# Sample attention in groups of four sequences, and later emission of norm multiplies, convolution steps and masked products, in a hybrid attention and state-space step

## The chip, the cores and the metric

The kernel runs on one core of one Trainium2 chip. The metric is the device time of one execution in microseconds; the median of runs counts.

## The reference

One layer of a decoder trunk with two groups of heads, on 512 prompt tokens and on 64 sample tokens (8 sequences of 8). Everything is fp32.

```python
h = rmsnorm(x, norm_pre)
q, k, v, g_a, z, xbc, dt = split(h @ w_in)
# group A: sliding-window attention (128), 32 query heads on 4 kv heads, a learned sink per head
o_a = attend(q, k, v, mask, sink)        # prompt: blocks of 128; sample: 128 cached keys + 8 new
attn_out = rmsnorm(o_a * silu(g_a), attn_norm)
# group B: Mamba-2 SSD
xbc = silu(causal_conv(xbc, conv_w, conv_b))         # width 4, depthwise
y, h_new = ssd(xs, dt, A, B, C, h0)                  # chunks of 128 with masked decay products
ssm_out = rmsnorm((y + d_skip * xs) * silu(z), ssm_norm)   # in 4 groups
out = concat(attn_out, ssm_out) @ w_out
return x + rmsnorm(out, norm_post), new caches and states
```

For the sample part, `swa_step` puts the 8 new keys behind the 128 cached ones; with T=8, W=128 query t sees key s where 0 <= t + 128 - s < 128. So of the cached keys it sees those with index above t, and of the new keys those with index up to t: always 128 keys.

## The kernel before

Tokens stand in columns: 512 prompt and 64 sample, 576 in two halves of 288; features stand in the 128 partitions. Every weight block (128 rows by 512 columns, a "unit") is loaded to one of 9 `raw` buffers, split into a high part (ACT cast, line 329) and a low part (DVE subtraction, line 332) in one of 4 `w` buffers, and used by `mm3` (lines 348 to 350): three fp32r matmuls, high by high, high by low, low by high. Where two column tiles are projected together (`pair`), seven products take the place of eight, with sums of weights made on POOL (line 269) and sums of results on DVE (lines 414 to 420).

The order is: x is normed while the first tiles are projected; the xBC tiles of four SSM groups and the z tiles; then for each of two rounds (pr = 0, 1; two kv heads each) k, v and eight pairs of q and gate tiles; then two output passes over w_out, the SSM half first, the attention half second. The projections are the dense work of TensorE. All else is side work.

The order of all instructions is made in advance. `Schedule` holds tasks written as generators; each `mm3` is a tick, and `yield n` means "go on n ticks later". A task emits its instructions at its tick into the in-order queues of the engines, and one DMA queue on SP takes all transfers. So a `yield` between a producer and its consumer sets how much other work stands ahead of the consumer on its engine; it is no wait in itself. If a task or a projection can get no buffer, it spends ticks until there is one. Buffers of 576 columns come from one pool (`slots`, with `smalls` a view on it), PSUM has 8 `banks`.

What the diff touches:

- `qb_task` (prompt attention, one call per head pair and half): scores, row maximum, exp, scaling, transposes, then ACT copies the transposed weights out of PSUM (line 1010) and DVE multiplies the same bank by a triangle mask (lines 1012 and 1014, the masked products), then the value matmuls (line 1024).
- `smp_task` (sample attention, one per round): loads of cached keys and values into four buffers; then `one(b)` for each of 8 sequences, at most three in flight. The kv heads stand in partition halves, so scores are 64-row matmuls for each half (lines 1067, 1068), two masked maxima with an additive mask tile (1074, 1075), exp (1081), scaling (1086), two transposes (1090, 1091), two copies (1094, 1095) and the value matmuls for each half, cached keys and new keys (1101, 1102) into one PSUM bank `osb` for all 8. At the end one multiplication by the gate for all (1115), stores to `m_d` and square sums.
- `renorm` (line 1129; called four times for the SSM groups and once for the 16 blocks of attention): `factors` loads the reciprocal norms (written to `r_d` by `Sums.finish`, 8 ticks before); then per block a load from `m_d` (1135), 8 ticks later the multiply on DVE (1137), one tick later the store (1139). The output passes read `m_d` (line 1544) once a block is ready.
- `conv_task` (line 1157, 24 calls): ACT makes the first tap (1163), three DVE steps add the others (1166), ACT tanh (1168), DVE finishes.
- `seq` inside `sample` (line 1374 on): the SSM state of a sequence is updated by DVE (1385) two ticks behind its matmul (1382).

Of the kernel before, what the change touches and what calls it, by code (L numbers as in the profile page):

```python
# [16 lines left out]
P = 128  # L17
# [161 lines left out]
def kern(ctx: ExitStack, tc: tile.TileContext, a: dict, o: dict):  # L179
# [15 lines left out]
    def const(name, shape):  # L195
        t = sb("c_" + name, shape)
        dma(t, a[name])
        return t
# [476 lines left out]
    masks = const("masks", [P, 640])  # L675
# [261 lines left out]
    def qb_task(st, jj, m, u):  # L937
# [72 lines left out]
        S.copy(pT[1][:, :512], pt)  # L1010
        if f:
# [5 lines left out]
        yield 9  # L1017
# [28 lines left out]
    def smp_task(st):  # L1046

        pr = st.pr
        own, ck, cv = [], [], []
        for h in range(2):  # L1050
            for src, dst in (("ckT", ck), ("cv", cv)):
                t = yield from smalls.get()
                own.append(t)
                dst.append(t[:, :512].rearrange("p (b k) -> p b k", b=4))
                dma(dst[h], a[src][pr, :, 4 * h:4 * h + 4])
        yield from wait(lambda: len(st.q) == 8 and st.kready and st.vready)
        if pr:
            yield 75
        osb = yield from banks.get()
        done = []  # L1060

        def one(b):
            sc = yield from banks.get()
            for hf in range(2):
                r0 = slice(64 * hf, 64 * hf + 64)
                lq = st.qs[r0, 64 * b:64 * b + 64]
                PE.matmul(sc[r0, 0:128], lq, ck[b // 4][r0, b % 4], start=True, stop=True)
                PE.matmul(sc[r0, 128:192], lq, st.kn[r0, TP:T], start=True, stop=True)
            yield 1
            pslot = yield from smalls.get()  # L1070
            p_ = pslot[:, :192]
            tn = yield from tiny.get()
            m0, mx, nm, den, es = (tn[:, k:k + 1] for k in range(5))
            V.tensor_tensor_reduce(p_[:, :128], sc[:, :128], masks[:, :128], 1.0, -3e38, ALU.add, ALU.max, m0)
            V.tensor_tensor_reduce(p_[:, 128:], sc[:, 128:192], masks[:, 128 + 64 * b:192 + 64 * b], 1.0, m0,
                                   ALU.add, ALU.max, mx)
            banks.put(sc)
            V.scalar_tensor_tensor(nm, mx, -0.125, nsinks[:, pr:pr + 1], op0=ALU.mult, op1=ALU.min)
            V.tensor_tensor(es, nm, sinks[:, pr:pr + 1], ALU.add)
            yield 3  # L1080
            S.activation(p_, p_, AF.Exp, bias=nm, scale=0.125, accum_out=den)
            S.activation(es, es, AF.Exp)
            yield 3
            V.tensor_tensor(den, den, es, ALU.add)
            V.reciprocal(den, den)
            V.tensor_scalar(p_, p_, den, None, op0=ALU.mult)
            tiny.put(tn)
# [721 lines left out]
```

## Time and profile before

| | us |
|---|---|
| median of 3 runs | 1655.22 (1653.7 to 1661.37) |
| profiled execution | 1653.8 |
| its span | 1652.0 |
| PE busy in it | 1598.8 (97%) |
| DVE busy | 1095.8 (66%) |
| ACT busy | 771.1 (47%) |
| POOL busy | 389.4 (24%) |

A matmul's time runs from its start to its modelled end and overlaps the next one's, so times of single matmuls do not add up; the step from start to start does. PEclk is the granted TensorE clock as a share of 2.4 GHz; it is either 1 or one half at any moment, and a figure between is a mean over the stretch. A wait is put down to the last releaser.

### The profile page before, as it was taken

The page shows a single profiled execution, that of the slowest core. Times are in us where ns is not written, and L with a number is a line of the kernel's source. Part 1 is how long each engine was busy: PE and PEld are TensorE (multiplying, and loading weights), DVE is VectorE, ACT ScalarE, POOL GpSimd, SP SyncE. Part 2 cuts the span into 40 slices and gives each one's busy share as a digit, 9 for nine tenths or more (in the row PEclk, how much of TensorE's full clock was granted, in tenths as well). Part 3 has the DMA queues.
Part 4 walks back from the last instruction along what each step waited for, and adds up shares of the span by engine and source line. Part 5 has one row for each costly group of instructions (what it writes and reads, how often), then busy time and mean ns, then how long its engine had stood idle before and what let it go on. Part 6 is the DMA issues. An engine that isn't in the chain of part 4 may idle for free.

```text
span 1652.0 us, 31869 instructions
## 1 busy us (share of the span) xinstructions
PE 1598.8 (97%) x12158; PEld 1542.6 (93%) x12158; DVE 1095.8 (66%) x2185; ACT 771.1 (47%) x1849; POOL 389.4 (24%) x420
## 2 busy tenths in 40 slices
PE   8999999999999999999999999999999999999995
PEld 8899999999989998998999999999899999999995
DVE  7656755775667567476778868777686455655556
ACT  6433433444434445364655636656573322544440
POOL 3201222221312220342223213222111211023323
PEclk9999999999999999999999999999999999999997
DMA  6324356546565648446314322323461356723235
GB/s 238 89 74 110 90 180 187 146 163 188 142 154 160 186 131 279 132 134 135 103 58 126 87 75 75 97 71 109 132 201 46 96 153 216 271 86 103 91 100 186
DMA packets 157977, 222.98 MB, mean 135 GB/s; under 512 B 32160, under 2 KB 66080, under 8 KB 157792
## 3 DMA queue, kind: packets, MB, share of 16 engines
q1 hardware_dynamic: 157824, 220.95, 44.5%
q8 instruction: 95, 1.56, 0.4%
q14 instruction: 58, 0.48, 0.1%
HBM read 182.26 MB, written 40.60 MB: 135 GB/s over the span
## 4 chain that ended last, share of the span: by engine, by line
PE 80%; DVE 8%; DMA 6%; ACT 2%; issue 2%; SPq 1%; POOL 0%; DVEq 0%; ACTq 0%; POOLq 0%
PE bank L348 23%; PE bank L350 23%; PE bank L349 22%; DMA s<-m_d 4%; PE bank L1024 2%; DVE w L332 1%; DMA r_d<-t 1%; DVE u L1166 1%; PE bank L1286 1%; PE bank L1003 1%; DMA s<-z_d 1%; PE bank L954 1%; PE bank L955 1%; PE bank L1298 1%; DVE s L1667 1%
## 5 line engine op out<-in xcount | busy, mean ns | idle before, releaser
L348 PE MATMUL bank<-x,w 128*128 128x288 f32 x3288 | 999.9, 304 | 6.4 <-DVE eT L420 2.6
L350 PE MATMUL bank<-x,w 128*128 128x288 f32 x3288 | 983.4, 299 | 17.2 <-DVE w L332 17.2
L349 PE MATMUL bank<-x,w 128*128 128x288 f32 x3288 | 980.6, 298 | 1.8 <-DVE x L542 1.8
L348 PEld LDWEIGHTS bank<-x,w 128*128 128x128 f32 x3288 | 625.7, 190 | 26.5 <-issue 15.1
L350 PEld LDWEIGHTS bank<-x,w 128*128 128x128 f32 x3288 | 626.8, 191 | 19.2 <-DVE w L332 19.2
L349 PEld LDWEIGHTS bank<-x,w 128*128 128x128 f32 x3288 | 625.8, 190 | 7.2 <-issue 3.8
L332 DVE TENSOR_TENSOR w<-raw,w 128x512 fp32r<-128x512 f32 x476 | 386.7, 818 | 130.4 <-ACT w L329 120.5
L329 ACT CAST w<-raw 128x512 fp32r<-128x512 f32 x476 | 289.4, 615 | 270.5 <-PE bank L349 226.0
L269 POOL TENSOR_TENSOR raw<-raw,raw 128x512 f32<-128x512 f32 x52 | 78.0, 1499 | 190.9 <-issue 163.3
L1166 DVE SCALAR_TENSOR_TENSOR u<-u,c_convwb,u 128x600 f32<-128x600 f32 x72 | 67.4, 940 | 24.0 <-ACT u L1163 22.9
L269 POOL TENSOR_TENSOR raw<-sum,raw 128x512 f32<-128x512 f32 x26 | 33.8, 1300 | 182.2 <-DVE w L332 171.2
L991 ACT ACTIVATE m<-m,t 128x128 f32<-128x128 f32 x128 | 49.9, 391 | 38.7 <-DVE t L986 38.7
L1236 ACT ACTIVATE m<-m,a_tok 128x128 f32<-128x128 f32 (+1 forms) x160 | 53.3, 381 | 19.3 <-DMA m<-aT_d 19.3
L998 ACT ACTIVATE m<-m,t 128x128 f32<-128x128 f32 x128 | 41.0, 392 | 45.5 <-DVE t L995 45.4
L542 DVE TENSOR_TENSOR x<-s,x 128x288 fp32r<-128x288 f32 x112 | 48.4, 479 | 18.9 <-ACT x L537 18.6
L830 POOL TENSOR_TENSOR s<-s,s 128x512 f32<-128x512 f32 (+2 forms) x42 | 46.0, 1096 | 56.2 <-ACT s L828 55.6
L1379 POOL TENSOR_TENSOR m<-m,dch 128x512 f32<-128x512 f32 x32 | 38.0, 1216 | 89.4 <-PE bank L1401 47.4
L1631 POOL TENSOR_TENSOR s<-s,s 128x288 f32<-128x288 f32 x28 | 23.0, 825 | 149.1 <-ACT s L1628 149.1
L269 POOL TENSOR_TENSOR sum<-raw,raw 128x512 f32<-128x512 f32 x26 | 35.5, 1366 | 94.1 <-DMA raw<-in_win_dram 56.1
L1272 POOL TENSOR_TENSOR m<-m,de 128x512 f32<-128x512 f32 (+1 forms) x20 | 25.3, 1264 | 112.9 <-DVE m L1265 96.7
L1163 ACT ACTIVATE u<-u,c_convwb 128x600 f32<-128x600 f32 x24 | 21.2, 889 | 65.5 <-DVE u L443 61.7
L1434 POOL TENSOR_TENSOR s<-s,s 128x576 f32<-128x576 f32 x16 | 24.8, 1552 | 98.2 <-DMA s<-z_d 88.2
(254 smaller groups left out, 1766.8 us busy)
## 6 DMA issues: line engine op xcount, KB each, us to landing
raw<-in_win_dram SPq DMA_DIRECT2D x304, 256.0 KB
raw<-in_wout_dram SPq DMA_DIRECT2D x128, 256.0 KB
s<-m_d SPq DMA_DIRECT2D x80, 288.0 KB
m_d<-s SPq DMA_DIRECT2D x48, 288.0 KB
s<-in_xT_dram SPq DMA_DIRECT2D x40, 288.0 KB
m<-aT_d SPq DMA_DIRECT2D x32, 256.0 KB
m<-in_h0T_dram SPq DMA_DIRECT2D x32, 256.0 KB
out_ss_dram<-m SPq DMA_DIRECT2D x32, 256.0 KB
```

The source lines that it names most:

```text
L269: G.tensor_tensor(dst, x, y, op)
L329: S.copy(w[:, 0], x)
L332: V.tensor_tensor(w[:, 1], x, w[:, 0].bitcast(F32), ALU.subtract)
L348: PE.matmul(out, w[:, 0, c], x[:, 0], start=start, stop=False, skip_group_check=True)
L349: PE.matmul(out, w[:, 0, c], x[:, 1], start=False, stop=False, skip_group_check=True)
L350: PE.matmul(out, w[:, 1, c], x[:, 0], start=False, stop=stop, skip_group_check=True)
L542: V.tensor_tensor(t[:, 1], src, t[:, 0].bitcast(F32), ALU.subtract)
L830: G.tensor_tensor(self.acc[:, c0:c0 + n], self.acc[:, c0:c0 + n], sq[:, :n], ALU.add)
L991: S.activation(p4[:, e], p4[:, e], AF.Exp, bias=nm[:, e:e + 1], scale=0.125, accum_out=den[:, e:e + 1])
L998: S.activation(p4[:, e], p4[:, e], AF.Copy, scale=den[:, e:e + 1])
L1166: V.scalar_tensor_tensor(y[:, :600], U[:, w:w + 600], cw[:, k, w:w + 1], y[:, :600], op0=ALU.mult, op1=ALU.add)
L1236: S.activation(Mv[q][:n, h, :n], Mv[q][:n, h, :n], AF.Relu, bias=a_tok[:n, c, k:k + 1], scale=-1.0)
```

## The change

Sample attention: `four(w)` takes the place of `one(b)`, for four sequences (w = 0, 1). `prepare` writes the queries block-diagonally (kv head 0 in the upper partitions of its 64 columns, kv head 1 in the lower ones, zero elsewhere), so that one 128-row matmul gives the scores of both kv heads; it appends the 8 new keys to the 128 cached ones (136 columns); and it subtracts from the 8 new value rows the first 8 cached ones. Query t sees either cached key j or new key j for j < 8, so after the scores the new ones with j <= t are copied over the first 8 columns (`sm8`), which leaves 128 keys; in the value product the difference of values, with the weights masked by `smT`, is added by a second matmul with 8 rows. Exp, scaling, transposes and copies work on four sequences at once. The second round starts after 60 ticks in place of 75. The additive mask tile is gone.

Emission: `renorm` gets a task of its own that loads up to four blocks ahead, each at least 26 ticks before its multiply. In `qb_task` the masked product comes 4 ticks after the ACT copy, and the value matmuls 8 ticks after it. In `conv_task` the steps are 6, 3, 3, 3 and 6 ticks apart in place of 3, 2, 2, 2 and 3, and only one convolution at a time is between its first tap and its last. In `seq` the update comes 5 ticks behind its matmul.

```diff
@@ -672,7 +672,9 @@
 
     mask1 = const("mask1", [P, P])
     later = mask1.bitcast(mybir.dt.uint32)
-    masks = const("masks", [P, 640])
+    sm8 = const("sm8", [P, 8])
+    own8 = sm8.bitcast(mybir.dt.uint32)
+    smT = const("smT", [8, P])
     nsinkb = const("sinkb", [P, 32])
     sinks = const("sinks", [P, 2])
     ii64 = const("ii64", [64, 32])
@@ -1008,13 +1010,14 @@
         pT4 = [t[:, :512].rearrange("p (f q k) -> p f q k", f=2, q=2) for t in pT]
 
         S.copy(pT[1][:, :512], pt)
+        yield 4
         if f:
             V.tensor_tensor(pT4[0][:, :, 1], ptv[:, :, 1], stri.unsqueeze(1).broadcast_to([P, 2, P]), ALU.mult)
         else:
             V.tensor_tensor(pT[0][:, :512].rearrange("p (e k) -> p e k", e=4), pt.rearrange("p (e k) -> p e k", e=4),
                             stri.unsqueeze(1).broadcast_to([P, 4, P]), ALU.mult)
         banks.put(pt)
-        yield 9
+        yield 8
         for q in range(2):
             qb = 2 * m + q
             w0 = 0 if qb else 1
@@ -1046,76 +1049,110 @@
     def smp_task(st):
 
         pr = st.pr
-        own, ck, cv = [], [], []
-        for h in range(2):
-            for src, dst in (("ckT", ck), ("cv", cv)):
-                t = yield from smalls.get()
-                own.append(t)
-                dst.append(t[:, :512].rearrange("p (b k) -> p b k", b=4))
-                dma(dst[h], a[src][pr, :, 4 * h:4 * h + 4])
+        ck, cv, qd, vd, slots_of = [], [], [], [], []
+        for w in range(2):
+            t = yield from slots.get()
+            ck.append(t[:, :544].rearrange("p (b k) -> p b k", b=4))
+            slots_of.append(t)
+            dma(ck[w][:, :, :P], a["ckT"][pr, :, 4 * w:4 * w + 4])
+            cv.append((yield from smalls.get()))
+            dma(cv[w][:, :512].rearrange("p (b k) -> p b k", b=4), a["cv"][pr, :, 4 * w:4 * w + 4])
         yield from wait(lambda: len(st.q) == 8 and st.kready and st.vready)
         if pr:
-            yield 75
-        osb = yield from banks.get()
+            yield 60
+        ms = yield from smalls.get()
+        msv = ms[:, :512].rearrange("p (h b t) -> p h b t", h=8, b=8)
+        sgv = st.sgs[:, :512].rearrange("p (h b t) -> p h b t", h=8, b=8)
         done = []
 
-        def one(b):
-            sc = yield from banks.get()
+        def prepare(w):
+
+            q = yield from smalls.get()
+            qd.append(q)
+            v = yield from smalls.get()
+            vd.append(v)
+            qv = q[:, :512].rearrange("p (b f r) -> p b f r", b=4, f=2)
+            for b in range(4):
+                dma(v[:8, P * b:P * b + P], vts[32 * w + 8 * b:32 * w + 8 * b + 8, pr])
             for hf in range(2):
                 r0 = slice(64 * hf, 64 * hf + 64)
-                lq = st.qs[r0, 64 * b:64 * b + 64]
-                PE.matmul(sc[r0, 0:128], lq, ck[b // 4][r0, b % 4], start=True, stop=True)
-                PE.matmul(sc[r0, 128:192], lq, st.kn[r0, TP:T], start=True, stop=True)
-            yield 1
+                G.memset(qv[r0, :, 1 - hf], 0.0)
+                G.tensor_copy(qv[r0, :, hf], st.qs[r0, 256 * w:256 * w + 256].rearrange("p (b r) -> p b r", b=4))
+            G.tensor_copy(ck[w][:, :, P:136], st.kn[:, TP + 32 * w:TP + 32 * w + 32].rearrange("p (b t) -> p b t", b=4))
+            yield 12
+            V.tensor_tensor(v[:8, :512], v[:8, :512], cv[w][:8, :512], ALU.subtract)
+
+        def four(w):
+            yield from prepare(w)
+            yield 6
+            qv = qd[w][:, :512].rearrange("p (b r) -> p b r", b=4)
+            sc = yield from banks.many(2)
+            scv = [t[:, :272].rearrange("p (b k) -> p b k", b=2) for t in sc]
+            for b in range(4):
+                PE.matmul(scv[b // 2][:, b % 2], qv[:, b], ck[w][:, b], start=True, stop=True)
+            smalls.put(qd[w])
+            slots.put(slots_of[w])
+            yield 2
             pslot = yield from smalls.get()
-            p_ = pslot[:, :192]
-            tn = yield from tiny.get()
-            m0, mx, nm, den, es = (tn[:, k:k + 1] for k in range(5))
-            V.tensor_tensor_reduce(p_[:, :128], sc[:, :128], masks[:, :128], 1.0, -3e38, ALU.add, ALU.max, m0)
-            V.tensor_tensor_reduce(p_[:, 128:], sc[:, 128:192], masks[:, 128 + 64 * b:192 + 64 * b], 1.0, m0,
-                                   ALU.add, ALU.max, mx)
-            banks.put(sc)
-            V.scalar_tensor_tensor(nm, mx, -0.125, nsinks[:, pr:pr + 1], op0=ALU.mult, op1=ALU.min)
-            V.tensor_tensor(es, nm, sinks[:, pr:pr + 1], ALU.add)
+            p4 = pslot[:, :512].rearrange("p (e k) -> p e k", e=4)
+            t1 = yield from tiny.get()
+            t2 = yield from tiny.get()
+            mx, nm, den, es = t1[:, 0:4], t1[:, 4:8], t2[:, 0:4], t2[:, 4:8]
+            for i in range(2):
+                S.copy(p4[:, 2 * i:2 * i + 2], scv[i][:, :, :P])
             yield 3
-            S.activation(p_, p_, AF.Exp, bias=nm, scale=0.125, accum_out=den)
+
+            for i in range(2):
+                V.copy_predicated(p4[:, 2 * i:2 * i + 2, :8], own8.unsqueeze(1).broadcast_to([P, 2, 8]), scv[i][:, :, P:136])
+            banks.put(*sc)
+            yield 2
+            V.tensor_reduce(mx, p4, mybir.AxisListType.X, ALU.max)
+            V.scalar_tensor_tensor(nm, mx, -0.125, nsinks[:, pr:pr + 1].broadcast_to([P, 4]), op0=ALU.mult, op1=ALU.min)
+            V.tensor_tensor(es, nm, sinks[:, pr:pr + 1].broadcast_to([P, 4]), ALU.add)
+            yield 4
+            for e in range(4):
+                S.activation(p4[:, e], p4[:, e], AF.Exp, bias=nm[:, e:e + 1], scale=0.125, accum_out=den[:, e:e + 1])
             S.activation(es, es, AF.Exp)
-            yield 3
+            yield 5
             V.tensor_tensor(den, den, es, ALU.add)
             V.reciprocal(den, den)
-            V.tensor_scalar(p_, p_, den, None, op0=ALU.mult)
-            tiny.put(tn)
+            yield 2
+            for e in range(4):
+                S.activation(p4[:, e], p4[:, e], AF.Copy, scale=den[:, e:e + 1])
+            tiny.put(t1, t2)
             yield 10
             pt = yield from banks.get()
-            PE.transpose(pt[:, 0:128], p_[:, 0:128], ident)
-            PE.transpose(pt[:TS, 128:256], p_[:, 128:192], ident)
+            for e in range(4):
+                PE.transpose(pt[:, P * e:P * e + P], p4[:, e], ident)
             yield 1
-            pT = yield from smalls.get()
-            S.copy(pT[:, 0:128], pt[:, 0:128])
-            V.tensor_copy(pT[:TS, 128:256], pt[:TS, 128:256])
+            pT = yield from smalls.two()
             smalls.put(pslot)
+            S.copy(pT[1][:, :512], pt)
+            V.tensor_tensor(pT[0][:8, :512].rearrange("p (e k) -> p e k", e=4), pt[:8].rearrange("p (e k) -> p e k", e=4),
+                            smT.unsqueeze(1).broadcast_to([8, 4, P]), ALU.mult)
             banks.put(pt)
-            yield 10
+            yield 9
+            po = yield from banks.get()
+            for b in range(4):
+                c = slice(P * b, P * b + P)
+                PE.matmul(po[:, c], cv[w][:, c], pT[1][:, c], start=True, stop=False)
+                PE.matmul(po[:, c], vd[w][:8, c], pT[0][:8, c], start=False, stop=True)
+            smalls.put(cv[w], vd[w], *pT)
+            yield from wait(lambda: len(st.sg) == 8)
+            yield 2
+
+            pov = po.rearrange("p (b f h t) -> p f h b t", b=4, f=2, h=8)
             for hf in range(2):
                 r0 = slice(64 * hf, 64 * hf + 64)
-                PE.matmul(osb[r0, TS * b:TS * b + TS], cv[b // 4][:, b % 4, r0], pT[:, r0], start=True, stop=False)
-                PE.matmul(osb[r0, TS * b:TS * b + TS], vts[:TS, pr, r0], pT[:TS, 128 + 64 * hf:192 + 64 * hf],
-                          start=False, stop=True)
-            smalls.put(pT)
-            done.append(b)
-
-        for b in range(8):
-            sch.spawn(one(b))
-            yield 7
-            yield from wait(lambda: len(done) > b - 2)
-        yield from wait(lambda: len(done) == 8 and len(st.sg) == 8)
-        yield 2
-
-        ms = yield from smalls.get()
-        V.tensor_tensor(ms[:, :512].rearrange("p (h b t) -> p h b t", h=8, b=8), st.sgs[:, :512].rearrange("p (h b t) -> p h b t", h=8, b=8),
-                        osb.rearrange("p (b h t) -> p h b t", b=8, h=8), ALU.mult)
-        banks.put(osb)
-        smalls.put(*own, st.qs, st.sgs)
+                V.tensor_tensor(msv[r0, :, 4 * w:4 * w + 4], sgv[r0, :, 4 * w:4 * w + 4], pov[r0, hf], ALU.mult)
+            banks.put(po)
+            done.append(w)
+
+        for w in range(2):
+            sch.spawn(four(w))
+            yield 24
+        yield from wait(lambda: len(done) == 2)
+        smalls.put(st.qs, st.sgs)
         slots.put(st.kn)
         yield 2
         for jj in range(8):
@@ -1129,13 +1166,23 @@
     def renorm(k0, row, gamma):
 
         Rt = yield from factors(row)
-        yield 10
-        for k in k0:
-            t = yield from slots.get()
-            dma(t, m_d[k])
-            yield 8
+        ahead, k0 = [], list(k0)
+
+        def load():
+            for k in k0:
+                yield from wait(lambda: len(ahead) < 4 and len(slots.free) > 5)
+                t = yield from slots.get()
+                dma(t, m_d[k])
+                ahead.append((k, t, sch.t + 26))
+                yield 8
+
+        yield 4
+        sch.spawn(load())
+        for _ in k0:
+            yield from wait(lambda: ahead and ahead[0][2] <= sch.t)
+            k, t, _ = ahead.pop(0)
             V.scalar_tensor_tensor(t, t, gamma[:, k % 16:k % 16 + 1], Rt, op0=ALU.mult, op1=ALU.mult)
-            yield 1
+            yield 3
             dma(m_d[k], t)
             yield 1
             slots.put(t)
@@ -1154,19 +1201,24 @@
             self.done = set()
             self.M, self.mid = {}, 0
 
+    conv_busy = [False]
+
     def conv_task(grp, name, box, k):
         U = box[0]
         Us = U[:, 515:603].rearrange("p (b w) -> p b w", w=11)
         G.tensor_copy(tails[:, k, 0], U[:, 512:515])
         G.tensor_copy(tails[:, k, 1:9], Us[:, :, 8:11])
+        yield from wait(lambda: not conv_busy[0])
+        conv_busy[0] = True
         y = yield from scratch.get()
         S.activation(y[:, :600], U[:, 0:600], AF.Identity, scale=cw[:, k, 0:1], bias=cw[:, k, 4:5])
-        yield 3
+        yield 6
         for w in range(1, 4):
             V.scalar_tensor_tensor(y[:, :600], U[:, w:w + 600], cw[:, k, w:w + 1], y[:, :600], op0=ALU.mult, op1=ALU.add)
-            yield 2
+            yield 3
+        conv_busy[0] = False
         S.activation(U[:, :600], y[:, :600], AF.Tanh)
-        yield 3
+        yield 6
         dst = yield from slots.get()
         V.scalar_tensor_tensor(dst[:, :TP], U[:, :TP], 1.0, y[:, :TP], op0=ALU.add, op1=ALU.mult)
 
@@ -1381,7 +1433,7 @@
             pS = yield from banks.get()
             PE.matmul(pS, Bs[:96], Xs[w][:96], start=True, stop=True)
             issued.add(b)
-            yield 2
+            yield 5
             V.tensor_tensor(h0[:, :512], h0[:, :512], pS, ALU.add)
             banks.put(pS)
             yield 2
```

`sm8[p, j]` is 1 where j <= p % 8, and `smT` is its transpose; they are made on the host with the other constants, in place of `masks`.

## Rows read from the trace of the kernel before

**Rows 1.** The page: busy time, share and instructions by engine; the chain by engine.
```profile
PE 1598.8 (97%) x12158; PEld 1542.6 (93%) x12158; DVE 1095.8 (66%) x2185; ACT 771.1 (47%) x1849; POOL 389.4 (24%) x420
...
PE 80%; DVE 8%; DMA 6%; ACT 2%; issue 2%; SPq 1%; POOL 0%; DVEq 0%; ACTq 0%; POOLq 0%
```
**Rows 2.** Who PE waited for: us in total, times, longest.
```profile
PE bank L350 <- DVE w L332: 17.2, 8, 3.9
```
**Rows 3.** Timeline of PE around one sequence: start, us, instruction, count.
```profile
943.52 0.29 PE L350 MATMUL bank<-x,w 128*128 128x288 f32 x1
943.74 0.33 PE L1101 MATMUL bank<-m,m 128*64 128x64 f32 x2
944.00 0.33 PE L1102 MATMUL bank<-m,vts 64*64 64x64 f32 x2
...
944.77 0.40 PE L348 MATMUL bank<-x,w 128*128 128x288 f32 x1
945.01 0.30 PE L349 MATMUL bank<-x,w 128*128 128x288 f32 x1
...
945.54 0.29 PE L350 MATMUL bank<-x,w 128*128 128x288 f32 x1
945.76 0.44 PE L1067 MATMUL bank<-m,m 64*64 64x128 f32 x4
...
946.49 0.30 PE L349 MATMUL bank<-x,w 128*128 128x288 f32 x1
```
**Rows 4.** Timeline of PE: four transposes of prompt attention, and one of sample attention.
```profile
942.01 0.60 PE L1003 MATMUL bank<-ident,m 128*128 128x128 f32 x4
...
946.75 0.27 PE L1090 MATMUL bank<-ident,m 128*128 128x128 f32 x1
```
**Rows 5.** Timeline of PE in an SSM scan: fp32 matmuls of 128 rows.
```profile
175.30 1.16 PE L1296 MATMUL bank<-s,m 128*128 128x128 f32 x8
176.29 1.02 PE L1298 MATMUL bank<-m,m 128*128 128x512 f32 x2
```
**Rows 6.** Timeline of PE in the dt stage, where the tile form changes.
```profile
94.00 0.41 PE L782 MATMUL bank<-c_tri,s 128*32 128x128 f32 x2
94.33 0.41 PE L779 MATMUL bank<-s,c_tri 128*128 128x32 f32 x2
```
**Rows 7.** Who DVE waited for: us in total, times, longest.
```profile
DVE s L1137 <- DMA s<-m_d: 71.4, 27, 7.5
DVE m L1014 <- ACT m L1010: 44.4, 15, 4.3
...
DVE u L1166 <- ACT u L1163: 22.9, 19, 7.2
```
**Rows 8.** Stretches: length, busy us of PE, PEld, DVE, ACT, POOL, granted clock, DMA share, GB/s.
```profile
460.00:480.00 20.00, 16.12 (x111) 15.88 (x110) 11.62 (x20) 6.02 (x15) 2.79 (x4) 0.91 0.70 187
630.00:650.00 20.00, 17.21 (x119) 16.75 (x119) 18.80 (x42) 12.92 (x32) 1.32 (x1) 0.83 0.82 263
755.00:775.00 20.00, 16.31 (x109) 15.62 (x109) 10.36 (x20) 8.75 (x26) 4.09 (x4) 0.83 0.66 210
...
1330.00:1390.00 60.00, 54.78 (x384) 53.94 (x383) 32.04 (x48) 16.07 (x28) 12.11 (x8) 0.94 0.65 200
925.00:990.00 65.00, 64.78 (x522) 58.87 (x521) 50.76 (x144) 30.77 (x95) 13.99 (x13) 1.00 0.31 93
```
**Rows 9.** Timeline of DVE in the attention norm; in brackets the idle time before.
```profile
1373.49 0.82 DVE L1137 SCALAR_TENSOR_TENSOR s<-s,c_ganorm,s 128x576 f32<-128x576 f32 x1 [2.82 <-DMA s<-m_d]
...
1382.40 0.82 DVE L1137 SCALAR_TENSOR_TENSOR s<-s,c_ganorm,s 128x576 f32<-128x576 f32 x1 [3.32 <-DMA s<-m_d]
```
**Rows 10.** Timeline of PE: three dense matmuls with waits in front.
```profile
764.45 0.61 PE L350 MATMUL bank<-x,w 128*128 128x288 f32 x1 [3.69 <-DVE w L332]
...
1195.55 0.40 PE L348 MATMUL bank<-x,w 128*128 128x288 f32 x1 [2.13 <-ACT x L537]
...
1341.00 0.37 PE L348 MATMUL bank<-x,w 128*128 128x288 f32 x1 [1.55 <-DVE eT L420]
```

More of the change, by code (lines that the diff above doesn't have):

```diff
@@ L1768, in lay_out @@
     a["mask1"] = np.where(j <= i, 0, NEG).astype(f)
-    t = (np.arange(P) % 8)[:, None]
-    b = np.arange(8)[:, None, None]
-    new = (sj // 8 == b) & (sj % 8 <= t)
-    new = new.transpose(1, 0, 2).reshape(P, 8 * TS)
-    a["masks"] = np.where(np.concatenate([j > t, new], 1), 0, NEG).astype(f)
+    a["sm8"] = (np.arange(8)[None, :] <= (np.arange(P) % 8)[:, None]).astype(f)
+    a["smT"] = a["sm8"].T
     return {k: np.ascontiguousarray(v) for k, v in a.items()}
```

## The prediction

> **What bounds the kernel now.** Four views were read in this order: the page's busy shares and its chain of waits; the list of who TensorE waited for; the instructions in order of time around the sample attention and around each long wait of TensorE; and the busy time by stretch, for the granted clock. The page says that PE is busy 97% of the span and holds 80% of the chain that ended last; DVE holds 8% of it [rows 1]. A busy PE is not yet a PE at its best, so the steps between starts were read. Dense matmuls follow each other by 0.1325 us (four steps from 945.01 to 945.54, [rows 3]), and this step is kept nearly everywhere. So PE's own instructions set the end, and a change counts only if it takes PE instructions away or takes away a wait of PE. The waits are few: eight times PE waited for the low half of a split weight (DVE, line 332), 17.2 us in all [rows 2]. DVE runs in order, so that line is late when something ahead of it on DVE waits: above all the norm multiply of line 1137, which waited 71.4 us in 27 places for its own load [rows 7]. After such a wait the granted clock is at its lower level, 1.2 instead of 2.4 GHz, for some microseconds: 0.91, 0.83 and 0.83 in the three 20 us stretches around the SSM norms, 0.94 over the attention norm [rows 8]. In the sample stage of the first round (925 to 990 us) it is 1.00.
>
> **Sample attention, PE.** Before, each of 8 sequences in each of 2 rounds has 8 score instructions (the trace has two for one fp32 call), 2 transposes and 8 value instructions. Scores: from the last dense start 945.54 to the second dense start behind, 946.49, is 0.95 us; less two dense steps (0.27) they cost 0.68. Values in the same way: 943.52 to 945.01 is 1.49, less 0.27 is 1.22. Transposes: 2 at 0.11, the step inside a run of four, (0.60 - 0.27)/3 [rows 3, 4]. Together 2.12 us, times 16: 33.9 us.
>
> After, there are 4 groups (2 rounds of 2). Scores: 8 instructions of 128 rows by 136 columns. The nearest row is the run of 8 at 128 columns, 175.30 to 176.29, 0.124 us each [rows 5]; times 136/128, times 8: 1.05, and 0.1 for the slower first dense step behind any run (0.24 at 945.01, [rows 3]). Transposes: 4 x 0.11 = 0.44. Values: 16 instructions, 4 sequences x (2 with 128 rows of weights, 2 with 8 rows). Eight-row weights do not occur in the trace. From below: the same 0.124 each, 2.0 us. From above: the run of lines 779 to 782, which changes its tile form, has 0.33 for a pair at its change of form (94.00 to 94.33, [rows 6]); eight pairs are 2.6 us. I take 2.3, between the two, and 0.1 behind. A group costs 1.15 + 0.44 + 2.4 = 4.0 us, four of them 16.0 (14.7 to 17.1). PE saves 17.9 us (16.8 to 19.2). Clock and cadence are full there, so this is time off the end.
>
> Alternating 128-row and 8-row weights is what a rule of the Trainium skill warns of ("TensorEngine Tiling (Array Packing)", section "Tiling Modes", Key Properties): a change of tiling mode, not merely of tile, drains TensorE. The trace shows little of a full drain: the value run of before changes form at every pair and takes 0.26 us for a pair, against 0.22 for two steps without a change [rows 3, 4]. If each of the eight pairs waited out one whole matmul (0.27 to 0.29 in the same rows) instead, values would cost about 3.1 us a group and the total would be 3 us higher.
>
> **Sample attention, other engines.** All of it lies beside PE. DVE loses 10 instructions a sequence (160 in all) and gains 11 a group (44), in a stage where it was busy 50.8 of 65 us; ACT keeps four a sequence in number (16 a group), some of them longer, and was busy 30.8; POOL gets five small fills and copies a group and was busy 14.0 [rows 8]. Four tiny loads a group go to SP's queue. I cost these at nothing with one exception: the new subtraction on v stands on DVE 12 ticks behind the issue of its loads (a tick is one triple of dense matmuls, 0.4 us, so 4.8 us). If SP is held up then, DVE waits with the weight split behind it. The bound is what line 1137 did with 8 ticks of lead: from no wait to 7.5 us [rows 7]. With 4 more ticks and loads of 4 KB I take 1 us of PE time per group, 4 us in all (0 to 14).
>
> **Norm multiplies.** The load used to be emitted 8 ticks (3.2 us) ahead of the multiply, now 26 (10.4 us), up to four loads ahead. The longest wait was 7.5 us [rows 7]; the chain in front of the first multiply of a group (store of the factors, broadcast load of the factors, then the load) is as long as before, but that multiply comes 12 ticks = 4.8 us later (38 in place of 26 behind the store), so up to 2.7 us of its wait remain. The later multiplies of a group lose their wait. What went with it on PE: of the 17.2 us in [rows 2], 2.19 belong to the start (72 us), 0.2 to the first matmuls and 0.8 to 330 us; the five others, 14.0 us, all stand behind line 1137, as the one of 3.69 at 764.45 does, and so does a sixth, of 1.55 behind an addition (line 420) at 1341 [rows 2, 10]. Sum 15.6 us. Clock: length times (1 - granted clock) in the four stretches of [rows 8]: 1.8 + 3.4 + 3.4 + 3.6 = 12.2 us. Together 27.8. Not all goes: waits of 2.82 us cost PE nothing at 1373 and one of 3.32 at 1382 stands ahead of a PE wait of 1.8 us and more clock [rows 9], so for the first multiplies of five renorms with up to 2.7 us I leave 5 us in (0 to 14). Gain 23 us (14 to 28). SP gains too: it no longer stands behind the stores that waited for these multiplies. The end of the attention norm is needed only by the second output pass; 8 ticks per block and an earlier sample stage do not make it later.
>
> **Convolutions and masked products.** The convolution steps stood 22.9 us for ACT and the masked products 44.4 us (line 1014 alone) for an ACT copy that was emitted just ahead of them [rows 7]. Nearly all of it was hidden: PE waited 0.8 us at 330 and 2.19 at 72 where conv steps were ahead of the split. Emitted later, they let the split go first. The convolution's own way gets 9 ticks (3.6 us) longer, 21 in place of 12, inside the 32 that one projection tile takes, so tiles do not pile up. I take 1 us of gain (-3 to +7: the start also ran at the lower clock).
>
> **Sum.** Against the profiled execution, 1653.8 us with a span of 1652.0: -17.9 (PE) -23 (norms) -1 (conv, mask) +4 (new subtraction) = -38, so 1616. The median of the three runs is 1.4 above that execution; 1617 by it.
>
> **Rivals.**
> A. The waits move instead of going. The emission order fixes every in-order queue; 26 ticks help only if SP issues on time, and it may stand behind weight loads that wait for a free buffer. Then DVE waits elsewhere, PE and its clock lose as much as before, and only the PE instructions count: 1655 - 18 = 1637. For it: waits of similar size arose from quite different releasers (2.13 us for an ACT cast at 1195, [rows 10]). Against it: five of the eight have one and the same cause, which is addressed directly.
> B. The edit does not bring what it says, because the new value runs drain at each change and the subtraction waits at its upper bound: PE saves 15, loses 14 and clock with it, norms gain only 14 of 28 and lose it again to first multiplies; about 1650 to 1655, no change.
> C. Slower: buffers run out. The grouped attention holds more tiles at once (query block, value difference, product, two transposed tiles) out of the same pool from which projections and output parts are taken. When a take finds none, the program's clock ticks on without dense matmuls, and PE then meets a row of dependent steps with nothing between. The nearest row is the start of the output passes, where the first operands are waited for in this way: 2.13 us [rows 10], and with the 3.4 us that the clock took after the wait at 764 [rows 8] some 5.5 us. Up to six such places only eat into the gain of 38; from seven on the kernel is slower; ten, over the two sample stages and the takes that follow, give 1617 + 55 = 1672. Against it: the group frees its query block and keys right behind the scores, and at most two groups are in flight.
>
> **How the numbers follow.** The forecast case (1600 to 1630) 0.62, A (1630 to 1645) 0.22, B 0.06, C 0.08, and 0.02 for better than 1600. For the range I take 1600 to 1642: from all bounds of the gains at their good end to A with some of its cost. What a measurement of this kernel can tell from no change is about 0.5%, 8 us. Faster by more than that 0.86, within 0.06, slower 0.08.
>
> **What would show it.** Right: 112 PE instructions in the sample attention (4 x 28) in place of 288 (16 x 18), line 1137's successor waiting under 25 us in all with no PE wait over 2 us behind it, granted clock near 1.00 around 470, 640, 765 and 1380 us. Wrong: value runs above 2.6 us a group, PE waits for the weight split as many as before but in other places (A), or PE idle with no releaser but ACT or DVE work of the sample attention, around the two sample stages (C).

## The result and the profile after

| | before | after |
|---|---|---|
| median, us | 1654.7 (4 runs) | 1605.4 (4 runs) |
| span of the profiled execution, us | 1652.0 | 1605.7 |
| predicted | | 1617 (1600 to 1642) |

The ratio is 0.9696 (95% interval 0.9672 to 0.972), 50 us less; the forecast was 38 less. One execution of a kernel below, after without the norm part, took 8631 us and stays out of its ratio. The page of after has the same shape, with PE at 98% and the chain more on PE (88% for 80%, [rows 1]):

```profile
PE 1572.0 (98%) x11982; PEld 1524.0 (95%) x11982; DVE 1081.4 (67%) x2067; ACT 771.9 (48%) x1849; POOL 393.6 (25%) x440
...
PE 88%; DVE 4%; ACT 3%; DMA 2%; issue 2%; SPq 1%; POOL 0%; DVEq 0%; ACTq 0%; POOLq 0%
```

Who PE waited for, after (us in total, times, longest). The wait for the weight split fell from 17.2 [rows 2] to 1.7 us; all of PE's waits in that view add up to 18.6, those of before to 38.3.

```profile
PE bank L350 <- DVE w L332: 1.7, 2, 1.5
```

Who DVE waited for, after. Line 1184 is the norm multiply (1137 before), 1217 the convolution step (1166), 1015 a masked product (1012): 71.4, 22.9 and 28.0 us before ([rows 7] has the first two, the third is below), now 2.2, 13.7 and 0.3; the other masked product (1014) waits no more.

```profile
DVE u L1217 <- ACT u L1214: 13.7, 15, 1.2
...
DVE s L1184 <- DMA s<-m_d: 2.2, 1, 2.2
...
DVE m L1015 <- ACT m L1012: 0.3, 1, 0.3
```

```profile
DVE m L1012 <- ACT m L1010: 28.0, 15, 2.2
```

DVE did not stop waiting: the weight split itself now waits longer for its own cast on ACT (line 329), first before, then after. PE's waits for the split, 1.7 us, show that this lies beside PE's work.

```profile
DVE w L332 <- ACT w L329: 127.0, 96, 4.2
```

```profile
DVE w L332 <- ACT w L329: 196.8, 158, 7.5
```

Stretches of after that hold the same work as those of [rows 8] (length, busy us by engine, granted clock third from the end). The clock is 1.00 in all of them.

```profile
460.00:480.00 20.00, 20.00 (x156) 18.90 (x155) 17.58 (x33) 9.64 (x23) 6.05 (x13) 1.00 0.51 167
600.00:660.00 60.00, 54.85 (x415) 51.29 (x414) 43.03 (x83) 32.88 (x76) 10.06 (x7) 1.00 0.76 238
740.00:780.00 40.00, 40.00 (x323) 38.98 (x322) 33.89 (x61) 23.10 (x68) 12.73 (x11) 1.00 0.50 167
...
1280.00:1370.00 90.00, 90.00 (x678) 90.00 (x677) 53.81 (x86) 29.79 (x56) 14.06 (x10) 1.00 0.71 237
```

One group of the sample attention in after, on PE (start, us, instruction, count), to be read as [rows 3]:

```profile
925.89 0.29 PE L350 MATMUL bank<-x,w 128*128 128x288 f32 x1
926.02 1.09 PE L1092 MATMUL bank<-s,m 128*128 128x136 f32 x8
926.86 0.38 PE L348 MATMUL bank<-x,w 128*128 128x288 f32 x1
927.08 0.29 PE L349 MATMUL bank<-x,w 128*128 128x288 f32 x1
...
937.31 0.30 PE L350 MATMUL bank<-x,w 128*128 128x288 f32 x1
937.45 0.39 PE L1138 MATMUL bank<-m,m 128*128 128x128 f32 x2
937.77 0.48 PE L1139 MATMUL bank<-m,m 8*128 8x128 f32 x2
938.18 0.49 PE L1138 MATMUL bank<-m,m 128*128 128x128 f32 x2
938.60 0.48 PE L1139 MATMUL bank<-m,m 8*128 8x128 f32 x2
939.01 0.49 PE L1138 MATMUL bank<-m,m 128*128 128x128 f32 x2
...
940.67 0.40 PE L348 MATMUL bank<-x,w 128*128 128x288 f32 x1
940.91 0.30 PE L349 MATMUL bank<-x,w 128*128 128x288 f32 x1
```

By the same reading as before: scores 925.89 to 927.08, less two dense steps, 0.92 us; values 937.31 to 940.91, less 0.27, 3.33; transposes 0.44. A group is 4.69 us, four are 18.8, so PE saves 15.1 of its 33.9 us. Values are above the upper bound of the prediction.

### The profile page after: what moved, and what is told of

It is laid out like the page before. It is cut to its first block, busy times and chain, and to the rows that moved or that the text cites. A ratio compares the mean times of both kernels' runs of the same rounds, so it can differ in the third digit from the quotient of the medians.

```text
span 1605.7 us, 31503 instructions
## 1 busy us (share of the span) xinstructions
PE 1572.0 (98%) x11982; PEld 1524.0 (95%) x11982; DVE 1081.4 (67%) x2067; ACT 771.9 (48%) x1849; POOL 393.6 (25%) x440
## 4 chain that ended last, share of the span: by engine, by line
PE 88%; DVE 4%; ACT 3%; DMA 2%; issue 2%; SPq 1%; POOL 0%; DVEq 0%; ACTq 0%; POOLq 0%
PE bank L348 26%; PE bank L349 25%; PE bank L350 25%; PE bank L1027 2%; PE bank L1338 1%; PE bank L956 1%; PE bank L957 1%; PE bank L1005 1%; PE bank L1350 1%; DVE s L1719 1%; DMA r_d<-t 1%; PE bank L1348 1%; DVE w L332 1%; PE bank L1453 0%; DMA s<-z_d 0%
## 5 line engine op out<-in xcount | busy, mean ns | idle before, releaser
L348 PEld LDWEIGHTS bank<-x,w 128*128 128x128 f32 x3288 | 621.0, 189 | 20.6 <-issue 16.3
L1217 DVE SCALAR_TENSOR_TENSOR u<-u,c_convwb,u 128x600 f32<-128x600 f32 x72 | 63.8, 886 | 14.3 <-ACT u L1214 13.7
L830 ACT ACTIVATE s<-s 128x512 f32<-128x512 f32 (+1 forms) x27 | 17.7, 656 | 78.1 <-DVE s L1037 42.9
```

The source lines that it names most:

```text
L348: PE.matmul(out, w[:, 0, c], x[:, 0], start=start, stop=False, skip_group_check=True)
L1217: V.scalar_tensor_tensor(y[:, :600], U[:, w:w + 600], cw[:, k, w:w + 1], y[:, :600], op0=ALU.mult, op1=ALU.add)
```

## The experiments

Theory: the parts gain separately, and what counts is PE's own instructions, PE's waits, and the clock behind them. Rival: the emission order is one knot, in which a wait that is removed comes up elsewhere. All times are medians; ratios are to the kernel before.

| run | us | ratio (95%) |
|---|---|---|
| sample attention alone | 1645.7 | 0.9944 (0.9923 to 0.9965) |
| norms alone | 1627.7 | 0.9838 (0.9818 to 0.9858) |
| convolutions alone | 1636.6 | 0.9891 (0.9872 to 0.9909) |
| masked product and state update alone | 1651.3 | 0.9971 (0.9957 to 0.9985) |
| after without the sample part | 1616.8 | 0.9765 (0.9747 to 0.9782) |
| after without the norm part | 1628.4 | 0.9827 (0.9808 to 0.9846) |
| after without the convolution part | 1607.9 | 0.9719 (0.97 to 0.9738) |
| after, value calls in another order (one product drops out, see below) | 1598.1 | 0.9658 (0.9635 to 0.9681) |
| the same with one opening call | 1598.0 | 0.9653 (0.9636 to 0.9669) |
| and the factors loaded later | 1596.5 | 0.9644 (0.9627 to 0.9661) |
| convolution steps apart, no lock | 1647.7 | 0.9951 (0.9935 to 0.9967) |
| after without the norm part, for its trace | 1628.05 | one run |

**Sample attention alone** (`smp_task` and its two masks from after, all else from before).

```diff
-        def one(b):
+        def prepare(w):
+        def four(w):
...
-            yield 75
+            yield 60
```

> The kernel before with the grouped sample attention alone. Theory (parts add, TensorE's own time counts): the steps in the trace of after give 0.84 + 0.36 + 3.23 us a group and 0.1 behind each run, 18.9 us in place of 33.9, so 15 us less, about 1640 against 1655. Rival (waits move, everything is one knot): the new emission order of the sample stage makes waits of its own, and the gain is under 5 us.

1645.7, 9 us less by the ratio, between the two. PE's instructions are as many as in after, but its waits grew in the attention norm, which now ran earlier (why they grew was not tried):

```profile
PE bank L350 <- DVE w L332: 19.6, 9, 4.1
```

That is 2.4 us more than [rows 2]: in the attention norm there are four of 1.2 to 3.3 us in place of two of 1.8. The clock falls behind one value run of this kernel as well, without a wait of PE there, 1.7 us (0.11 x 15):

```profile
955.00:970.00 15.00, 14.83 (x93) 13.62 (x92) 10.86 (x22) 6.51 (x19) 5.13 (x4) 0.89 0.42 132
```

So the part comes with waits, and the rival is right to that extent.

**Norms alone.**

```diff
-            dma(t, m_d[k])
-            yield 8
...
+                yield from wait(lambda: len(ahead) < 4 and len(slots.free) > 5)
+                t = yield from slots.get()
+                dma(t, m_d[k])
+                ahead.append((k, t, sch.t + 26))
+                yield 8
...
+            yield from wait(lambda: ahead and ahead[0][2] <= sch.t)
```

> The kernel before with the new renorm alone (loads up to four ahead, 26 ticks before the multiply). Theory: the waits behind the norm multiply go, 23 us of waits and lower clock, about 1632; the PE waits for the weight split at 469, 635, 760, 1354 and 1382 us are gone and the clock there is 1.00. Rival: other instructions take the place ahead of the split on DVE, and under 8 us are won.

1627.7, 27 us less. The waits and the low clock of [rows 8] are gone together. Who PE waited for, and the four stretches of [rows 8], with the norms alone:

```profile
PE bank L350 <- DVE w L332: 2.4, 2, 2.2
```

```profile
460.00:480.00 20.00, 20.00 (x158) 19.14 (x156) 15.45 (x28) 8.07 (x18) 3.71 (x7) 1.00 0.79 245
630.00:650.00 20.00, 20.00 (x162) 19.77 (x161) 18.77 (x42) 13.86 (x28) 0.00 (x0) 1.00 0.90 311
755.00:775.00 20.00, 20.00 (x161) 19.67 (x161) 19.19 (x36) 11.53 (x33) 6.57 (x5) 1.00 0.37 117
1330.00:1390.00 60.00, 60.00 (x453) 60.00 (x452) 36.87 (x61) 21.02 (x41) 6.92 (x5) 1.00 0.72 240
```

**Convolutions alone.**

```diff
+        yield from wait(lambda: not conv_busy[0])
+        conv_busy[0] = True
...
-        yield 3
+        yield 6
...
-            yield 2
+            yield 3
+        conv_busy[0] = False
...
-        yield 3
+        yield 6
```

> The kernel before with the new conv_task alone (steps further apart, one convolution at a time). The prediction gave it 1 us; the traces of before and after part by some 10 us already before 100 us, where only convolutions differ. Theory now: 8 us less, about 1647, with the PE waits at 70 and 72 us gone and the clock near 1.00 from 73 to 81 us. Rival: the start differs for another reason, and the time stays within 3 us of before.

1636.6, 18 us less: more than the theory said. From 70 to 110 us, before and with the convolutions alone, in that order:

```profile
70.00:110.00 40.00, 35.30 (x219) 33.04 (x218) 25.34 (x59) 12.31 (x23) 2.02 (x15) 0.83 0.33 84
```

```profile
70.00:110.00 40.00, 40.00 (x303) 38.58 (x302) 28.91 (x64) 17.32 (x35) 3.99 (x13) 1.00 0.36 91
```

The start gives 4.7 us of waits and 0.17 x 40 = 6.8 us of clock, 11.5 us. The rest is in the norms, and why a change of the convolutions shortens waits there was not tried: the wait at 469 us is 0.7 us where it was 3.9, and PE's waits for the split are 6.2 us in all:

```profile
PE bank L350 <- DVE w L332: 6.2, 7, 2.3
```

Of the clock at the start one trace says little. The kernel after and the second of the two with sorted value calls (below) are the same program up to that point, and PE waits in neither; yet after lost 3.6 us of clock in these 40 us, and the sorted one nothing (after, then sorted):

```profile
70.00:110.00 40.00, 40.00 (x280) 38.56 (x280) 27.58 (x60) 14.89 (x31) 3.43 (x10) 0.91 0.32 84
```

```profile
70.00:110.00 40.00, 40.00 (x303) 38.58 (x302) 28.92 (x64) 17.34 (x34) 4.47 (x15) 1.00 0.34 91
```

**Masked product and state update alone.**

```diff
         S.copy(pT[1][:, :512], pt)
+        yield 4
...
-        yield 9
+        yield 8
...
-            yield 2
+            yield 5
             V.tensor_tensor(h0[:, :512], h0[:, :512], pS, ALU.add)
```

> The kernel before with the masked product 4 ticks later (value matmuls 3 ticks later) and the state update 5 ticks behind its matmul in place of 2. Theory: DVE's waits at lines 1012 and 1014 (72 us) fall by more than half but lay beside TensorE's work: at most 3 us less, 1652 to 1655. Rival: these waits held up weight splits in the attention stage, and 8 us or more are won.

1651.3, 4.8 us less (2.5 to 7.1), between theory and rival. DVE's waits at the two masked products fell from 72 to 0.3 us, so they were nearly all covered.

**After without one part.** The edits are those above, the other way round.

> After, with the sample attention of before. Theory (TensorE's own time is off the end): 15 us more than after's 1605.4, about 1620. Rival (alone it gave 9 us, so it gives 9 here too): about 1614; in the run with the sample part alone the attention norm's waits grew, and with the new renorm in place nothing of that kind should be left, so the theory says that the full 15 shows here.

> After, with the renorm of before. If the parts were independent, 27 us more, about 1632. Theory: the convolution part alone had already made the waits of the SSM norms shorter (0.7 and 1.3 us in place of 3.9 and 2.8), so the two overlap and the loss is smaller, 12 to 20 us, about 1617 to 1625.

> After, with the convolution emission of before. Theory: what only the convolutions win is the start (waits of 1.5, 2.2 and 1.0 us at 70, 72 and 92 us and the lower clock there, 6.8 us), 11 us more than after, about 1616. Rival (the parts add): 18 us more, about 1623.

Against after's ratio the sample part is worth 0.0069 of 1655, 11 us; the norms 0.0131, 22; the convolutions 0.0023, 4, which is not clear of nothing. The four parts alone add up to 59 us, together they give 50. So the parts overlap, the convolutions most (alone 18, here 4): without them the start's waits are back (PE, 74 and 77 us),

```profile
73.96 0.40 PE L348 MATMUL bank<-x,w 128*128 128x288 f32 x1 [1.55 <-ACT w L329]
...
76.69 0.61 PE L350 MATMUL bank<-x,w 128*128 128x288 f32 x1 [2.20 <-DVE w L332]
```

but after has four waits of 1.0 to 1.5 us from 607 to 645 us, 5.0 us, that the kernel without them doesn't have; it has only one there, of 0.6. The sample part's 11 us are fewer than the 15.1 read off PE's steps; the next runs bear on why.

**Another order of the value calls.** The 128-row calls of a group first, then the 8-row calls. In the first of the two kernels the value product over the cached keys drops out of the sum; that this comes of four 128-row calls that each open the bank anew is argued from the second kernel, which differs in that alone. The second kernel is the one in the diff: only one call opens the bank.

```diff
             for b in range(4):
                 c = slice(P * b, P * b + P)
-                PE.matmul(po[:, c], cv[w][:, c], pT[1][:, c], start=True, stop=False)
-                PE.matmul(po[:, c], vd[w][:8, c], pT[0][:8, c], start=False, stop=True)
+                PE.matmul(po[:, c], cv[w][:, c], pT[1][:, c], start=b == 0, stop=False, skip_group_check=True)
+            for b in range(4):
+                c = slice(P * b, P * b + P)
+                PE.matmul(po[:, c], vd[w][:8, c], pT[0][:8, c], start=False, stop=b == 3, skip_group_check=True)
```

> After, with the value matmuls of a group in another order: the four calls with 128 rows of weights first, then the four with 8 rows, so the tile form changes twice a group and not eight times. Theory (the change of form drains the array): the run falls from 3.2 us to about 2.2, 4 us less in all, about 1601.5. Rival (weights of 8 rows are slow by themselves): the run stays at 3.2 us and the time at 1605.

> After, with the four value calls of 128 rows first and the four of 8 rows behind them, and only the first of them opening the bank. Theory (the change of tile form drains the array): as in the run with the other order, value runs of 2.07 us in place of 3.23, 4.6 us less in all, 1598 to 1601. Rival: the second form of accumulation changes the steps, and the run is back at 3.2 us.

Both 1598, 7 us under after by the ratio of the second kernel (some 2 to 12, an estimate from the two intervals). The run of values in it:

```profile
932.91 0.30 PE L350 MATMUL bank<-x,w 128*128 128x288 f32 x1
933.05 1.06 PE L1138 MATMUL bank<-m,m 128*128 128x128 f32 x8
934.03 1.16 PE L1141 MATMUL bank<-m,m 8*128 8x128 f32 x8
935.12 0.40 PE L348 MATMUL bank<-x,w 128*128 128x288 f32 x1
935.35 0.29 PE L349 MATMUL bank<-x,w 128*128 128x288 f32 x1
```

Less two dense steps it is 2.17 us in place of 3.33: 4.6 us for four groups. Eight rows of weights cost 0.136 us a step (934.03 to 935.12), 128 rows 0.123, so the rival falls: it is the change of form. A pair in after's alternating run takes 0.41 us against 0.25 (128 rows) or 0.27 (8 rows) for two steps, and the whole run 1.15 us more for six changes more: 0.14 to 0.19 us for each change. That an 8-row call adds to the columns just written is not the reason: the step behind it, to a 128-row call on other columns, costs the same (0.42 and 0.41 from 938.18 on). The rest fits the clock, 2.5 us, though the interval of the 7 us could hold without it. Behind one value run of each round after's granted clock goes to its lower level although PE never waited in that run; with the calls sorted it stays up. The stretch behind a value run in each round, after, then with the calls sorted:

```profile
935.00:950.00 15.00, 15.00 (x95) 14.03 (x94) 7.58 (x19) 6.06 (x19) 4.19 (x3) 0.89 0.55 161
1225.00:1240.00 15.00, 15.00 (x95) 14.03 (x94) 7.08 (x17) 7.49 (x22) 1.30 (x1) 0.89 0.07 18
```

```profile
930.00:945.00 15.00, 15.00 (x116) 14.76 (x115) 9.29 (x22) 7.50 (x21) 4.53 (x3) 1.00 0.60 180
...
1215.00:1230.00 15.00, 15.00 (x117) 14.76 (x116) 6.99 (x17) 8.57 (x24) 1.83 (x1) 1.00 0.01 3
```

Twice 0.11 x 15 is 3.3 us. It does not happen behind every such run: in the four traces with alternating calls (after, the sample part alone, after without the convolutions, after without the norms) the clock fell behind 6 of 16 value runs, in the three with sorted calls behind none of 12. So the sample part is 15.1 of PE steps less 3.3 of clock, 11.8, by after's trace; the run without it gave 11. In full, the two traces differ by 15.1 of steps and 2.1 of PE waits, less 3.3 of clock here and 3.6 at the start (where the kernel without the part has 1.00), which is 10.3, and their spans by 10.6.

**Factors loaded later.** In after, SP stands until the small store of the factors has landed, and the decay loads behind it come late (SP, then ACT, start, us, idle before in brackets):

```profile
593.16 0.52 SPq L309 DMA_DIRECT2D raw<-in_win_dram  x1
603.16 0.33 SPq L847 DMA_DIRECT2D s<-r_d  x1
603.58 0.93 SPq L1277 DMA_DIRECT2D m<-aT_d  x2
```

```profile
608.46 0.40 ACT L1288 ACTIVATE m<-m,a_tok 128x128 f32<-128x128 f32 x1 [8.18 <-DMA m<-aT_d]
```

```diff
         yield from sums.finish(4 * 512, 1 + g)
-        yield 8
+        yield 26
...
         yield from sumA.finish(4 * D, 0)
-        yield 8
+        yield 26
```

> The same as the run with the order and one opening call, and the broadcast load of the factors emitted 26 ticks behind the store of the factors in place of 8. In after SP stands up to 9.3 us in front of that load until the store has landed (38.7 us in 6 waits), and the decay loads emitted behind it come late: at 607 us ACT waits 8.2 us for one and TensorE 1.3 us for the cast behind it. Theory: SP's waits there fall under 10 us in all and TensorE's waits near 607 to 619 us go, 2 to 5 us less than the run with the order alone. Rival: those waits are DVE's and ACT's own load at that place, and nothing is won.

SP's waits in front of that load fell from 35.9 us (with the order alone) to 6.3, with 5.2 us for the same store now in front of another load, and PE's waits from 607 to 620 us went. But one at 644 us of 2.5 us came up, and 1596.5 against 1598.0 is no difference that these intervals show. Nothing was won, as the rival said. Whether the later load made the new wait is not shown: the first of the two sorted kernels, which loads as after does, has one of 2.5 us at 649 us.

**Convolution steps apart, without the lock.** The diff is to the kernel with the convolutions alone.

```diff
-        yield from wait(lambda: not conv_busy[0])
-        conv_busy[0] = True
```

> The kernel before with the steps of the convolutions further apart, but several convolutions at a time as before. With the one-at-a-time rule the part gave 18 us. Theory A (the distance of the steps lets evacuations and weight splits go between them): nearly all of it, 1636 to 1640, the start's waits at 70 and 72 us gone. Theory B (at the start two convolutions stand ready at once, and what helps is that they no longer run interleaved): the waits at 70 and 72 us stay, and 6 us or less are won.

1647.7, 8 us less: neither theory. The waits at 70 and 72 us did go by the distance alone (0.4 us is left), but PE then waited 3.26 us at the dt stage for the end of a chain of small DVE operations, and the clock fell further than before (0.74):

```profile
88.13 0.64 PE L779 MATMUL bank<-s,c_tri 128*128 128x32 f32 x2 [3.26 <-DVE s L770]
```

```profile
70.00:110.00 40.00, 36.17 (x204) 33.11 (x203) 21.48 (x53) 10.37 (x20) 2.31 (x15) 0.74 0.32 78
```

With the lock that chain ends no earlier (89.15 against 88.08 us), but PE comes to it behind its end (convolutions alone):

```profile
88.83 0.32 DVE L770 SCALAR_TENSOR_TENSOR s<-dt,s 128x160 f32<-128x160 f32 x1
```

```profile
90.38 0.30 PE L779 MATMUL bank<-s,c_tri 128*128 128x32 f32 x2
```

So the start is won by both together. What is won without the lock is not in the start: PE's waits for the split are 7.0 us in place of 17.2, most of the difference in the norms.

**The norm part left out, seen in its trace.**

> The kernel of the run with the renorm of before in after, once more, for its trace (the first trace fell on a disturbed execution). Its loss of 22 us should show as TensorE waits for the weight split behind the norm multiply and as lower clock after them: if it does, at least three waits of over 1.5 us between 460 and 1380 us that after does not have, the one near 469 us short as in the run with the convolutions alone, and some 18 to 22 us of waits and clock. If the loss is of another kind (SP standing in front of stores, weights late), the waits would name DMA or the ACT cast.

1628.05 once. Who PE and who DVE waited for:

```profile
PE bank L350 <- DVE w L332: 17.6, 9, 4.5
```

```profile
DVE s L1174 <- DMA s<-m_d: 77.9, 29, 10.6
```

Line 1174 is the norm multiply here. The split's waits are back (15.9 us more than in after), with 8.5 us of clock behind the waits at 611, 748 and 1301 us (0.83, 0.83 and 0.89 over 20, 20 and 15 us); at 469 us the split waits no more. That is 24.4 us; less the 3.6 of clock that after lost at its start and this execution did not, 20.8. The spans differ by 20.6 us.

## Why the prediction was right, and where its sizes were off

The time lies in the range, and the mechanism held. That it came within 12 us of the forecast is in part luck: terms were missed in both directions.

- What bounds the kernel: right. PE at a fixed step, its waits behind the in-order DVE, and the clock behind the waits carry the whole difference.
- Sample attention on PE: the mechanism was right (PE's instructions fell by 176, the forecast 288 less 112), the term too large, 17.9 for 15.1. The wrong choice was the price of values: the text took 2.3 us a group and bounded it at 2.6 from a row with 32-column and 128-column forms. It was 3.22 (937.45 to 940.67) and the first dense step behind it, so one of the prediction's signs of being wrong, value runs above 2.6 us a group, came true. The sentence there that let every pair wait out one matmul, worked from rows, came nearer with 3.1 us a group and 3 us more in all, and the sorted calls show that the change of form is what costs. The Trainium skill ("TensorEngine Tiling (Array Packing)", section "Tiling Modes", Key Properties) says that a change of tiling mode drains TensorE. The traces agree that such a change costs time, but not one time for all: 0.14 to 0.19 us between 128 and 8 rows here, 0.04 between the forms of the value run before (0.26 for 0.22). And the clock that fell behind two alternating runs, 3.3 us, was not thought of: the text said that the clock is full there, from the trace of the kernel before.
- The new subtraction and its loads (4 us): nothing. DVE never waited for it, and no wait of PE stands behind it.
- Norm multiplies: right. 23 us (14 to 28) was said; 27 alone, 22 within after. The sum of waits and clock read from before, 27.8, was nearly all won when nothing else was changed; the 5 us left in for the first multiplies were not needed: DVE waits 2.2 us in all for such a load in after.
- Convolutions and masked products: mis-sized, 1 us (-3 to +7). Alone the convolutions gave 18 and the masks 5; within after the convolutions give 4 or less. The step that failed was to price the start by its waits (2.2 us at 72) and leave the clock there, 6.8 us in the trace of before, to the upper end of the range; it stands in the same kind of row that was used for the norms. The 7 us that the convolutions alone win in the norms were not thought of.
- The whole, from the two traces: PE's waits 38.3 - 18.6 = 19.7 us; PE's steps in the sample attention 15.1; lower clock (1 - 0.981) x 1652 - (1 - 0.990) x 1606 = 15. That is 50, against 46 of span (lower clock while PE waits is in it twice). What the forecast of 38 lacked is, by these readings, the start, the masked products and the 4 us taken off for the subtraction, and what it had too much is in the sample part.
- Rival A (waits move) fell for the norms, but holds in small: in the sample part alone, around 640 us, and perhaps when the factors were loaded later. Rival B had its first term right (PE saves 15, because the value runs pay at each change), and fell with the others. Rival C fell: the one wait of its kind in that view of PE is 0.5 us, for the masked product of the grouped attention.

The best version is after with the value calls sorted, 1598.0, ratio 0.9653; after itself is 0.9696, and the intervals just part. What still makes the small waits around 640 us is open, and so is which of the later state update and the later masked product gave the 5 us; neither was tried.

## What to carry to other kernels

Where one engine runs at a fixed step, add to each of its waits the clock that is lost behind it: here 12.2 us behind 15.6 us of waits in the norms, 6.8 beside 4.7 at the start, and the second pair was missed. Such clock differs by some 3 us between executions of the same instructions, so one trace does not price it to the microsecond. In an in-order queue an operation that waits for a load should be emitted when the load has landed, not soon after it was issued: here 26 ticks ahead in place of 8 gave 27 us. Matmuls of different tile forms are better sorted than alternated: here 7 us.

## What was not expected of the hardware

A run of 16 fp32 matmuls that changes between 128-row and 8-row weights costs 0.14 to 0.19 us at each change, and behind 6 of 16 such runs the granted clock fell to 1.2 GHz (0.89 over 15 us) though PE was never without work in the run; behind 12 runs of the same 16 sorted it stayed at 2.4 GHz. Eight rows of weights are no cheaper than 128 (0.136 and 0.123 us). A load of the factors, issued behind their store of some 2 KB, held the one DMA queue for up to 9.3 us until the store had landed.
